# A hybrid trunk layer on one core: the decay's chain of small VectorE operations emitted in five pieces, p read in quarters with a third place, the second half's residual loaded later

## The chip, the core and the metric

The kernel runs on one core of a Trainium2 chip. A core has five engines, each with an instruction stream of its own that it works through in order: TensorE (PE, the matrix products, with its weight loads shown apart as PEld), VectorE (DVE), ScalarE (ACT), GpSimd (POOL) and SyncE (SP, which here only issues transfers). ACT issues transfers too, and sixteen DMA engines carry them between DRAM and the on-chip memory. The metric is the device time of one execution in microseconds; less is better. The kernel before takes 1365.46 us (median of three runs, 1364.79 to 1365.91).

## What is computed

One layer of a decoder trunk over 1024 tokens and 1024 channels, all in float32. The attention group and the gated DeltaNet group read one input projection, their outputs go through `w_o`, and an MLP and a gated embedding follow:

```
u = rmsnorm(h, norm_mix[i])
aq, ak, av, dq, dk, dv, dz, db, da = split(u @ w_in[i])
attn_out = sliding_window_sink_attention(rope(aq), rope(ak), av, sinks)
beta = sigmoid(db)
g = -exp(a_log) * softplus(da + dt_bias)              # the decay
dn_out = chunk_gated_delta_rule(l2norm(silu(conv(dq))) * 128 ** -0.5, l2norm(silu(conv(dk))), silu(conv(dv)), g, beta)
dn_out = rmsnorm(dn_out) * dn_norm * silu(dz)
h = h + concat(attn_out, dn_out) @ w_o[i]
h = h + square(relu(rmsnorm(h, norm_mlp[i]) @ w_up[i])) @ w_down[i]
h = h + sigmoid(rmsnorm(h, norm_ple[i]) @ w_ple_gate[i]) * (p[i] @ w_ple_proj[i])
out = rmsnorm(h, norm_final)
```

## The kernel before

The tokens are worked on in two halves of 512 (`hb` 0 and 1). A product in full precision is made of three passes: each operand is split by `split` (L219 and L220) into a rounded part (a cast on ACT) and its difference to the source (on POOL or DVE), and PE multiplies high by high, high by low and low by high.

*Who sets the order.* Up to w_out, `Flow` writes out two kinds of work. The filler `projections()` is a generator of large GEMMs; the tasks (`prepare`, `chain`, `attend`, and `pairs` with its merges, preps and scans) are chains of small steps, each of which yields the time in microseconds, or the event, for which its next step has to wait. A task that is due goes first, the filler otherwise, and `embed()` is a spare filler for when the filler itself has to wait. That sequence gives the priorities; the scheduler of the tile framework then fixes each engine's own row of instructions by a timeline of its own. On the chip each engine keeps to its row, and an instruction that waits holds back all behind it.

*The decay.* `scalars(s, hb)` (L625 to L672) computes beta and g for a half on tiles of 128x16: some two dozen DVE operations and two exponentials on ACT, a chain in which each needs the one before, written in one piece up to a `yield 3.17`. Three small matmuls of `gg` follow. `norms` adds the l2 norms, and `pre` makes four decay steps: POOL writes `rD` (L724), PE multiplies it by `mgtR`, ACT takes the exponential into `et` (L735), POOL masks it (L737), and DVE multiplies the products of keys and queries by it into `ka` (L751). The key part goes to DRAM (`LD`, L757), comes back as `rD` (L770), and `inverse` (L764 to L784) runs 31 steps on DVE, from L775 to L780. Its result goes through DRAM (`XD`) to `Xt`; `merge` (from L802), `prep` and `scan` follow. The scan carries the state `St` over four chunks for two groups of heads; each link runs through PE, DVE, ACT and POOL, and ends with transposes of `oS` whose split is written to `AT` and `Z`. Two PSUM banks (pool d) serve the scans, three (pool e) all other steps, three (pool g) the filler. `z_gate` (L433 to L437) multiplies z by its silu and the norm's weights, on ACT and in four POOL instructions.

*The embed.* `embed()` (L1049 to L1077) makes p @ w_proj and writes it to the DRAM tensor `PD`. Half of p at a time lies in AT0, as high and low part; a tile of output is 12 matmuls, then ACT copies the bank into `po` (two buffers, L1072) and SP issues the write (L1075). The second half's p can be put into AT0 only when the first half's products are done.

*The residual.* `hT(hb, j)` is where x, transposed, is kept and added to: for the first half the end of `H`; for the second half's first four blocks the beginning of `H`, and AT1 for its last four. `w_out(hb)` begins with two transfers of 1 MB each, issued by ACT (L1006), and adds its products to these places at the end of each group of banks (L1024). For the second half, w_out begins with the part that doesn't need the scan.

Of the kernel before, what the change touches and what calls it, by code (L numbers as in the profile page):

```python
# [18 lines left out]
P = 128  # L19
# [99 lines left out]
def hybrid_block(ctx, tc, t, out):  # L119
# [6 lines left out]
    def nm(s):  # L126
        cnt[0] += 1
        return f"{s}{cnt[0]}"
# [498 lines left out]
    def scalars(s, hb):  # L627

        w = lambda name: dt_([P, 16], name, bufs=2)
        z = ba[:, hb * 4:hb * 4 + 4]  # L630
        v44 = lambda x: x.rearrange("p (t h) -> p t h", t=4)
        beta = w("beta")
        A.activation(v44(beta), z[:, :, 0:4], AF.Exp, scale=-1.0)
        V.tensor_scalar(beta, beta, 1.0, None, op0=ALU.add)
        V.reciprocal(beta, beta)
        a_, e_, f_, g_ = w("sa"), w("se"), w("sf"), w("gg")
        V.tensor_tensor(v44(a_), z[:, :, 4:8], bc(dtb, 1, 4), op=ALU.add)
        V.tensor_scalar(e_, a_, -1.0, None, op0=ALU.mult)
        V.tensor_tensor(e_, e_, a_, op=ALU.min)
        V.tensor_scalar(a_, a_, 0.0, None, op0=ALU.max)  # L640
        A.activation(e_, e_, AF.Exp)

        V.tensor_scalar(f_, e_, 2.0, None, op0=ALU.add)
        V.reciprocal(f_, f_)
        V.tensor_tensor(e_, e_, f_, op=ALU.mult)
        V.tensor_tensor(f_, e_, e_, op=ALU.mult)
        V.tensor_scalar(g_, f_, 1.0 / 17.0, None, op0=ALU.mult)
        for i in (15, 13, 11, 9, 7, 5, 3):
            V.scalar_tensor_tensor(g_, g_, 1.0 / i, f_, op0=ALU.add, op1=ALU.mult)  # L649
        V.scalar_tensor_tensor(g_, g_, 1.0, e_, op0=ALU.add, op1=ALU.mult)  # L650
        V.scalar_tensor_tensor(g_, g_, 2.0, a_, op0=ALU.mult, op1=ALU.add)
        V.tensor_tensor(v44(g_), v44(g_), bc(nea, 1, 4), op=ALU.mult)
        gh = dt_([P, 16], "gh", bufs=2, dt=F32R)
        gl = dt_([P, 16], "gl", bufs=2, dt=F32R)
        A.copy(gh, g_)
        V.tensor_tensor(gl, g_, gh.bitcast(F32), op=ALU.subtract)
        yield 3.17
        b, free = yield from take("e")
        for i, m in enumerate((mle, mgtR.bitcast(F32), ones)):
            T.matmul(b[:, i * 16:i * 16 + 16], m, g_, start=True, stop=True)  # L660
        free()
        ex = dt_([P, 3, 16], "ex", bufs=2)
        A.activation(ex, b[:, 0:48].rearrange("p (i t) -> p i t", i=3), AF.Exp)
        s.update(beta=beta, gh=gh, gl=gl, eG=ex[:, 0], eR=ex[:, 1], eL=ex[:, 2],
                 ss=dt_([P, 2, 16], "ss", bufs=2), KE=[None] * 4, AT=[None] * 4)
        s["LD"] = dram.tile([64, 1024], F32, tag="LD", name=nm("LD"), bufs=2)
        s["XD"] = XD[hb]
        s["BD"] = dram.tile([16, P], F32, tag="BD", name=nm("BD"), bufs=2)
# [330 lines left out]
    def hT(hb, j, n=1):  # L999

        x, o = (H, XW + j * HB) if hb == 0 else (H, j * HB) if j < 4 else (AT[1], (j - 4) * HB)
        return x[:, o:o + n * HB]

    def w_out(hb):
        for j in (0, 4):
            A.dma_start(hT(hb, j, 4).rearrange("p (j s) -> p j s", j=4),  # L1006
                        t["xT"].rearrange("(j p) s -> p j s", p=P)[:, j:j + 4, hb * HB:hb * HB + HB])

        def rhs(b, kt):
            return dn1[b][:, kt - 4] if hb and kt > 3 else uview(R1, b, kt)  # L1010
# [37 lines left out]

    def embed():  # L1049

        for hb in range(2):
            pT = part("AT0", F32R).rearrange("p (b k s) -> p b k s", b=2, k=2)
            for kt in range(2):
                raw = wraw.tile([P, WN], F32, tag="raw", name=nm("pr"))[:, :HB]
                SY.dma_start(raw, t["pT"][kt * P:(kt + 1) * P, hb * HB:(hb + 1) * HB])
                split(pT[:, 0, kt], pT[:, 1, kt], raw, G)
            for g in range(4):
                w = wunit2(t["w_proj"], 0, g * 256, G)
                for m in range(0, 4, 2):
                    ring["g"].n -= 1  # L1060
                    b = bank(ps["g"])
                    for kt in range(2):
                        for i in range(2):
                            for j, (x, y) in enumerate(PASSES):
                                T.matmul(b[:, i * 256:i * 256 + 256],
                                         pT[:, x, kt, (m + i) * P:(m + i + 1) * P],
                                         w[:, y, kt * 256:kt * 256 + 256],
                                         start=kt + i + j == 0, stop=kt * i == 1 and j == 2)
                            if kt + i < 2:
                                yield  # L1070
                    o = cvp.tile([P, HB], F32, tag="cv", name=nm("po"))
                    A.copy(o, b)  # L1072
                    ring["g"].n += 1
                    r = hb * HB + m * P
                    SY.dma_start(PD[r:r + 2 * P, g * 256:g * 256 + 256].rearrange("(i p) c -> p i c", p=P),  # L1075
                                 o.rearrange("p (i c) -> p i c", i=2))
                    yield  # L1077
# [528 lines left out]
```

## Time and profile before

| | |
|---|---|
| median of three runs | 1365.46 us |
| the profiled execution | 1366.2 us, its span 1364.1 us |
| PE busy | 1317.7 us, 97% |
| DVE, ACT, POOL busy | 838.8, 548.0, 434.5 us (61%, 40%, 32%) |
| chain that ended last | PE 74%, DVE 11%, DMA 6%, ACT 3%, POOL 2% |
| decay of the first half, first keys and attention | 50 to 132 us |
| embed, decay steps of the second half | 385 to 448 us |
| w_out, the second half's inverse and scan | 448 to 600 us |

The times of the trace are microseconds from the start of the span. A timeline row gives start, duration, engine, line, operation, what is written and read, and in brackets how long the engine stood idle before it and who released it. Each engine is busy for only part of the time; an idle stretch counts where PE has it. PEclk is the granted clock of PE as a share of 2.4 GHz: 1.00 is the upper level, 0.50 the lower one, 1.2 GHz; a stretch that has both shows a value between.

### The profile page before, as it was taken

The numbers are of one execution on the slowest core, as the hardware profiler recorded it, in microseconds if no ns is written. First come the engines' busy times: TensorE is split into PE (matmuls) and PEld (weight loads), VectorE is DVE, ScalarE is ACT, GpSimd is POOL, SyncE is SP. The second block draws the span as 40 slices with busy tenths as digits, with TensorE's granted clock in tenths as the row PEclk, the third lists the DMA queues.
The fourth block names the chain that finished last, engine by engine and source line by source line (L and its number), as shares of the span: only waits on it lengthen the run. The fifth ranks groups of instructions, "written<-read, shape, count | busy, mean of one in ns | idle before, by whom it ended". The sixth has DMA issues, their size and how long they took to land.

```text
span 1364.1 us, 20392 instructions
## 1 busy us (share of the span) xinstructions
PE 1317.7 (97%) x7664; PEld 1125.5 (83%) x7664; DVE 838.8 (61%) x1558; ACT 548.0 (40%) x1083; POOL 434.5 (32%) x430
## 2 busy tenths in 40 slices
PE   8999999999998999898999999999999999999997
PEld 6788688999897998886788888877888888888886
DVE  6786977697564755797776676654333343344553
ACT  6456375544544433564333333342122231221333
POOL 6673626631385452300011111103122212210332
PEclk9999999999999999999999999999999999999999
DMA  6322222324135431321433323354333333232211
GB/s 223 88 54 73 54 62 52 74 73 105 34 119 176 133 110 33 115 85 63 146 116 116 124 87 114 109 185 136 96 116 101 98 123 120 77 93 73 75 62 47
DMA packets 102738, 134.33 MB, mean 98 GB/s; under 512 B 16400, under 2 KB 71744, under 8 KB 102384
## 3 DMA queue, kind: packets, MB, share of 16 engines
q1 hardware_dynamic: 90528, 110.50, 27.0%
q10 hardware_dynamic: 11760, 21.77, 4.4%
q8 instruction: 60, 0.98, 0.3%
q0 software_dynamic: 352, 0.76, 0.2%
q14 instruction: 38, 0.31, 0.1%
HBM read 106.77 MB, written 26.23 MB: 98 GB/s over the span
## 4 chain that ended last, share of the span: by engine, by line
PE 74%; DVE 11%; DMA 6%; ACT 3%; issue 3%; POOL 2%; SPq 1%; POOLq 0%; ACTq 0%; DVEq 0%
PE bk L102 72%; PE bk L106 2%; DVE w L220 1%; DVE cv L412 1%; DMA AD<-t 1%; ACT w L219 1%; DMA raw<-in_w_in 1%; POOL rsb L358 1%; DMA PD<-po 1%; DMA raw<-in_w_down 1%; DMA H<-in_w_in 1%; DMA AT<-in_xT 0%; DVE gg L649 0%; DMA raw<-AD 0%; SPq L841 0%
## 5 line engine op out<-in xcount | busy, mean ns | idle before, releaser
L102 PE MATMUL bk<-T,w 128*128 128x512 f32 x2304 | 537.9, 392 | 5.7 <-ACT w L219 4.5
L102 PEld LDWEIGHTS bk<-T,w 128*128 128x128 f32 x2304 | 432.8, 188 | 102.6 <-ACT w L219 6.6
L220 POOL TENSOR_TENSOR w<-raw,w 128x512 fp32r<-128x512 f32 x136 | 180.5, 1329 | 621.3 <-ACT w L219 590.2
L219 ACT CAST w<-raw 128x512 fp32r<-128x512 f32 (+1 forms) x280 | 172.6, 620 | 460.8 <-PE bk L102 340.6
L102 PE MATMUL bk<-R,w 128*128 128x256 f32 (+1 forms) x1536 | 240.7, 312 | 1.4 <-ACT w L219 1.4
L102 PEld LDWEIGHTS bk<-R,w 128*128 128x128 f32 x1536 | 210.8, 189 | 22.9 <-issue 2.3
L220 DVE TENSOR_TENSOR w<-raw,w 128x512 fp32r<-128x512 f32 (+1 forms) x144 | 107.5, 748 | 61.1 <-ACT w L219 60.9
L1478 DVE TENSOR_TENSOR H<-bk,H 128x512 f32<-128x512 f32 x96 | 64.6, 690 | 96.0 <-PE bk L102 96.0
L102 PE MATMUL bk<-U,w 128*128 128x512 f32 (+1 forms) x384 | 80.3, 355 | 1.0 <-ACT ba L472 0.6
L102 PEld LDWEIGHTS bk<-U,w 128*128 128x128 f32 x384 | 60.2, 191 | 14.5 <-issue 4.9
L102 PE MATMUL bk<-w,R 128*128 128x256 f32 (+1 forms) x480 | 69.4, 294 | 0.1
L102 PE MATMUL bk<-w,U 128*128 128x256 f32 (+2 forms) x384 | 64.1, 321 | 5.2 <-ACT AT L478 3.2
L102 PE MATMUL bk<-AT,w 128*128 128x256 f32 (+1 forms) x256 | 65.3, 342 | 1.3 <-DVE t L1363 0.8
L102 PEld LDWEIGHTS bk<-w,U 128*128 128x128 f32 x384 | 55.6, 194 | 12.3 <-ACT AT L478 3.4
L102 PEld LDWEIGHTS bk<-w,R 128*128 128x128 f32 x480 | 61.7, 192 | 4.0 <-issue 3.1
L1348 ACT ACTIVATE t<-t 128x512 f32<-128x512 f32 x64 | 40.3, 631 | 39.1 <-DVE t L1347 38.4
L102 PEld LDWEIGHTS bk<-AT,w 128*128 128x128 f32 x256 | 42.8, 191 | 8.3 <-DVE t L1363 1.9
L102 PE MATMUL bk<-R,T 128*128 128x512 f32 (+1 forms) x204 | 48.7, 386 | 0.0
L220 POOL TENSOR_TENSOR T<-ra,T 128x1024 fp32r<-128x1024 f32 x14 | 33.6, 2398 | 46.7 <-ACT T L219 41.0
L102 PE MATMUL bk<-T,T 128*128 128x512 f32 (+1 forms) x204 | 47.0, 379 | 0.0
L555 ACT ACTIVATE s<-s,mx 128x257 f32<-128x257 f32 (+1 forms) x64 | 31.3, 492 | 36.8 <-DVE mx L553 30.2
L102 PEld LDWEIGHTS bk<-T,T 128*128 128x128 f32 x204 | 36.8, 188 | 7.8
(370 smaller groups left out, 1882.1 us busy)
## 6 DMA issues: line engine op xcount, KB each, us to landing
raw<-in_w_in SPq DMA_DIRECT2D x72, 256.0 KB, 2.8
raw<-in_w_up SPq DMA_DIRECT2D x32, 512.0 KB, 4.9
AD<-t ACTq DMA_DIRECT2D x64, 256.0 KB, 2.7
raw<-in_w_down SPq DMA_DIRECT2D x64, 256.0 KB, 3.0
ra<-AD SPq DMA_DIRECT2D x28, 512.0 KB, 4.1
raw<-in_w_o SPq DMA_DIRECT2D x32, 256.0 KB, 3.1
PD<-po SPq DMA_DIRECT2D x16, 256.0 KB, 3.7
rawg<-in_w_gate SPq DMA_DIRECT2D x16, 256.0 KB, 3.2
```

Source lines behind the costliest of these rows:

```text
L102: self.tc.nc.tensor.matmul(o, lh, rh, **k)
L106: self.tc.nc.tensor.transpose(o, x, i)
L219: A.copy(hi, src)
L220: lo_eng.tensor_tensor(lo, src, hi.bitcast(F32), op=ALU.subtract)
L358: eng.tensor_tensor(acc, acc, xr, op=ALU.add)
L412: V.scalar_tensor_tensor(cv if i < 3 else x[:, 3:], x[:, i:i + HB], cw[:, j, i:i + 1], cv, op0=ALU.mult, op1=ALU.add)
L555: A.activation(s[:, i, lo:257], s[:, i, lo:257], AF.Exp, bias=mx[:, i:i + 1], accum_out=sm[:, i:i + 1])
L1348: A.activation(r, r, AF.Square)
L1478: V.tensor_tensor(h, bs[m], h, op=ALU.add)
```

## The change

Three places of the code change. The decay's chain in `scalars` gets four yields of 1.5 us, so that it is written out in five pieces with other work between. p comes in four quarters of 256 tokens; two lie in AT0, the third in a tile of its own (`pT`), the fourth in the first's place; the third is read ahead of the first half's third group of w_proj, the fourth ahead of the second half. For the second half's residual, an 8-column copy on ACT is put ahead of the transfers: it reads a block of the first half's residual and writes into the block to be loaded, so the transfer into `H` waits for that block's first addition, and AT1's transfer is written first.

```diff
@@ scalars
         V.reciprocal(beta, beta)
+        yield 1.5
         a_, e_, f_, g_ = w("sa"), w("se"), w("sf"), w("gg")
...
         A.activation(e_, e_, AF.Exp)
+        yield 1.5
...
         for i in (15, 13, 11, 9, 7, 5, 3):
             V.scalar_tensor_tensor(g_, g_, 1.0 / i, f_, op0=ALU.add, op1=ALU.mult)
+            if i in (13, 7):
+                yield 1.5
@@ w_out
+    def x_in(hb, j):
+        A.dma_start(hT(hb, j, 4).rearrange("p (j s) -> p j s", j=4),
+                    t["xT"].rearrange("(j p) s -> p j s", p=P)[:, j:j + 4, hb * HB:hb * HB + HB])
+
     def w_out(hb):
-        for j in (0, 4):
-            A.dma_start(hT(hb, j, 4).rearrange("p (j s) -> p j s", j=4),
-                        t["xT"].rearrange("(j p) s -> p j s", p=P)[:, j:j + 4, hb * HB:hb * HB + HB])
+        if hb:
+            A.copy(hT(1, 0)[:, 0:8], hT(0, 1)[:, 0:8])
+        for j in (4, 0)[::1 - 2 * (hb == 0)]:
+            x_in(hb, j)
@@ embed
+        two = part("AT0", F32R).rearrange("p (i b s) -> p i b s", i=2, b=2)
+        extra = dx.tile([P, 2, HB], F32R, tag="pT", name="pT")
+        places = [two[:, 0], two[:, 1], extra, two[:, 0]]
+        def quarter(i):
+            raw = wraw.tile([P, WN], F32, tag="raw", name=nm("pr"))[:, :HB]
+            SY.dma_start(raw.rearrange("p (k s) -> p k s", k=2),
+                         t["pT"].rearrange("(k p) s -> p k s", p=P)[:, :, i * 256:i * 256 + 256])
+            split(places[i][:, 0], places[i][:, 1], raw, G)
+        quarter(0)
+        quarter(1)
         for hb in range(2):
-            pT = part("AT0", F32R).rearrange("p (b k s) -> p b k s", b=2, k=2)
-            for kt in range(2):
-                raw = wraw.tile([P, WN], F32, tag="raw", name=nm("pr"))[:, :HB]
-                SY.dma_start(raw, t["pT"][kt * P:(kt + 1) * P, hb * HB:(hb + 1) * HB])
-                split(pT[:, 0, kt], pT[:, 1, kt], raw, G)
+            if hb:
+                quarter(3)
             for g in range(4):
+                if hb == 0 and g == 2:
+                    quarter(2)
                 w = wunit2(t["w_proj"], 0, g * 256, G)
                 for m in range(0, 4, 2):
+                    pT = places[hb * 2 + m // 2]
```

What this does to the engines' rows shows in three places. On POOL, in the decay steps of the second half (`rD` and `et` are a step's tiles, `z` the gating), before:

```order
L724 TENSOR_TENSOR rD_4304<-con,gh_3433 128x512
L724 TENSOR_TENSOR rD_4304<-con,gl_3434 128x512
L944 TENSOR_TENSOR oss_4227<-oss_4227,mhalf 128x2
L437 TENSOR_TENSOR z_3396<-z_3396,rows 128x512 x4
L737 TENSOR_TENSOR et_4301<-et_4301,con 128x512
L220 TENSOR_TENSOR w_5195<-raw_5193,w_5195 128x512
L724 TENSOR_TENSOR rD_4489<-con,gh_3433 128x512
```

The same place on POOL after the change (L728, L741 and L948 are the lines of before, moved down by four):

```order
L728 TENSOR_TENSOR rD_4304<-con,gl_3545 128x512
L741 TENSOR_TENSOR et_4301<-et_4301,con 128x512
L220 TENSOR_TENSOR w_4935<-raw_4933,w_4935 128x512
L728 TENSOR_TENSOR rD_4489<-con,gh_3544 128x512
L728 TENSOR_TENSOR rD_4489<-con,gl_3545 128x512
L220 TENSOR_TENSOR w_4972<-raw_4970,w_4972 128x512
L948 TENSOR_TENSOR oss_4348<-oss_4348,mhalf 128x2
L437 TENSOR_TENSOR z_3396<-z_3396,rows 128x512 x4
L741 TENSOR_TENSOR et_4486<-et_4486,con 128x512
```

The gating stood ahead of the first step's `et`; now it stands ahead of the second's. On ACT, around the transfers into `H` (`x2` is two transfers in a row), before:

```order
L1072 COPY po_5262<-bk_5249 128x512
L959 COPY Z_79<-bk_4458 128x256
L219 CAST w_5325<-raw_5323 128x512
L219 CAST w_5452<-raw_5450 128x512
L1006 DMA H<-in_xT 128x4x512 x2
L913 ACTIVATE oS_4606<-bk_4607,ex_546 128x128 x2
```

The same place on ACT after the change (L739, L1009 and L1095 are L735, L1006 and L1072 of before):

```order
L739 ACTIVATE et_4799<-bk_4796 128x512
L219 CAST AT_4923<-pr_5240 128x512
L1095 COPY po_5216<-bk_5203 128x512
L1009 DMA H<-in_xT 128x4x512
L219 CAST w_5246<-raw_5244 128x512
```

The later transfer on ACT after the change, some thirty rows on in w_out (L1268 squares the first half's new residual, L1015 is the copy):

```order
L219 CAST w_5895<-raw_5893 128x512
L1268 ACTIVATE rsb<-H 128x512
L1015 COPY H<-H 128x8
L1268 ACTIVATE t_6901<-H 128x512
L1009 DMA H<-in_xT 128x4x512
```

One of the two transfers stays at the embed; the other has moved behind w_out's first residual. On PE, near the end of the second half's scan (`St` is the state, `oS` an output that is transposed, `bk_6199` and `bk_6233` the last chunk's banks of the first group of heads), before:

```order
L102 MATMUL bk_6087<-vn_6062,ka_4652 128x128 x2
L102 MATMUL bk_6416<-AT_5500,w_6629 128x256
L102 MATMUL bk_6417<-AT_5500,w_6629 128x256
L106 MATMUL bk_5951<-con,oS_5918 128x128 x2
L102 MATMUL bk_6199<-St_3391,W_6161 128x128 x2
L102 MATMUL bk_6199<-St_3391,xq_2846 128x128 x2
L106 MATMUL bk_6087<-con,oS_6056 128x128
L102 MATMUL bk_6233<-vn_6204,ka_4805 128x128 x2
```

The same links of the scan on PE after the change (just ahead of these rows stand the product of `bk_6087` and five more w_o matmuls):

```order
L102 MATMUL bk_6478<-R_75,w_6541 128x256
L106 MATMUL bk_5951<-con,oS_5918 128x128
L102 MATMUL bk_6478<-R_75,w_6541 128x256
L106 MATMUL bk_5951<-con,oS_5918 128x128
L102 MATMUL bk_6478<-R_75,w_6541 128x256 x4
L102 MATMUL bk_6328<-AT_5500,w_6570 128x256
L102 MATMUL bk_6329<-AT_5500,w_6570 128x256
L102 MATMUL bk_6417<-AT_5500,w_6630 128x256
L102 MATMUL bk_6418<-AT_5500,w_6630 128x256
L102 MATMUL bk_6199<-St_3391,W_6161 128x128 x2
L102 MATMUL bk_6199<-St_3391,xq_2846 128x128 x2
L102 MATMUL bk_6233<-vn_6204,ka_4805 128x128 x2
```

Matmuls of w_out (`R` by `w`) now stand between the links, and the product with `vn` no longer stands behind a transpose of `oS`. The first merge of the second half, where this stretch begins, has 255 w_o matmuls ahead of it in PE's row instead of 321.

## Rows read from the trace of the kernel before

**Rows 1.** The page: busy us, share of the span, instructions of each engine.

```profile
PE 1317.7 (97%) x7664; PEld 1125.5 (83%) x7664; DVE 838.8 (61%) x1558; ACT 548.0 (40%) x1083; POOL 434.5 (32%) x430
```

**Rows 2.** Windows: us, PE, PEld, DVE, ACT, POOL busy, PEclk, DMA share, GB/s.

```profile
406.50:410.50 4.00, 4.00 (x22) 4.00 (x22) 3.17 (x7) 1.38 (x4) 1.32 (x1) 0.57 0.29 47
...
441.00:447.50 6.50, 4.13 (x19) 4.13 (x20) 2.90 (x6) 3.49 (x9) 3.21 (x3) 0.50 0.64 177
450.00:526.00 76.00, 76.00 (x763) 73.22 (x762) 48.76 (x127) 27.79 (x62) 35.40 (x30) 1.00 0.33 95
...
545.00:558.00 13.00, 8.42 (x54) 7.17 (x53) 7.14 (x25) 4.73 (x19) 3.36 (x4) 0.87 0.14 41
```

**Rows 3.** Timeline of PE: start, us, instruction, count [idle before it <- releaser].

```profile
63.43 0.40 PE L102 MATMUL bk<-gg,con 128*128 128x16 f32 x2 [0.60 <-DVE gg L652]
...
89.36 0.37 PE L106 MATMUL bk<-con,s 128*128 128x128 f32 x1 [2.98 <-DVE s L558]
...
406.30 1.56 PE L102 MATMUL bk<-xk 128*128 128x128 f32 x8 [2.03 <-DVE ka L751]
...
420.19 0.92 PE L102 MATMUL bk<-vn,ka 128*128 128x128 f32 x4 [2.52 <-ACT oS L913]
...
427.87 1.05 PE L102 MATMUL bk<-xk 128*128 128x128 f32 x8
...
443.37 5.10 PE L102 MATMUL bk<-w,AT 128*128 128x256 f32 x24 [3.77 <-ACT po L1072]
...
448.45 2.62 PE L102 MATMUL bk<-R,w 128*128 128x256 f32 x20
...
451.72 35.94 PE L102 MATMUL bk<-R,w 128*128 128x256 f32 x301
487.59 0.68 PE L102 MATMUL bk<-XT,ka 64*64 64x64 f32 x16
```

**Rows 4.** Timeline of POOL, first half's weights, then the second half's decay.

```profile
68.47 1.32 POOL L220 TENSOR_TENSOR w<-raw,w 128x512 fp32r<-128x512 f32 x1 [1.76 <-ACT w L219]
...
395.84 5.11 POOL L437 TENSOR_TENSOR z<-z,rows 128x512 f32<-128x512 f32 x4
400.90 1.30 POOL L737 TENSOR_TENSOR et<-et,con 128x512 f32<-128x512 f32 x1
```

**Rows 5.** Timeline of ACT (ACTq: a transfer that it issues).

```profile
392.06 1.28 ACT L735 ACT_TABLE_LOAD   x1
...
393.36 0.60 ACT L735 ACTIVATE et<-bk 128x512 f32<-128x512 f32 x1
...
430.07 0.98 ACTq L1006 DMA_DIRECT2D H<-in_xT  x2
```

**Rows 6.** Transfers from 424 to 450 us: issuer, count, KB each, us to landing.

```profile
H<-in_xT ACTq DMA_DIRECT2D x2, 1024.0 KB, 9.4
```

**Rows 7.** The tile po, 385 to 450 us: landing of its 14 writes.

```profile
DMA to landing us min/median/max: 2.1/3.4/10.1
```

**Rows 8.** Timeline of DVE: the inverse's start, a residual addition, the transpose.

```profile
446.69 1.22 DVE L775 TENSOR_TENSOR rD<-rD,bS 128x1024 f32<-128x1024 f32 x1
...
460.28 0.69 DVE L1024 TENSOR_TENSOR H<-bk,H 128x512 f32<-128x512 f32 x1 [1.11 <-PE bk L102]
...
486.31 0.45 DVE L802 STREAM_TRANSPOSE XT<-Xt 128x256 f32<-128x256 f32 x1 [1.83 <-DMA Xt<-XD]
```

**Rows 9.** Waits of PE from 526 to 560: us in total, times, longest.

```profile
PE bk L106 <- DVE oS L949: 2.3, 2, 1.2
PE bk L102 <- DVE kvs L858: 1.9, 2, 1.4
PE bk L102 <- DVE Z L220: 1.8, 2, 0.9
```

**Rows 10.** Timeline of SP's issues: the loads rD<-LD.

```profile
437.99 4.73 SPq L770 DMA_DIRECT2D rD<-LD  x2
```

More of the change, by code (lines that the diff above doesn't have):

```diff
@@ L1065, in embed @@
                                 T.matmul(b[:, i * 256:i * 256 + 256],
-                                         pT[:, x, kt, (m + i) * P:(m + i + 1) * P],
+                                         pT[:, x, kt * 256 + i * P:kt * 256 + i * P + P],
                                          w[:, y, kt * 256:kt * 256 + 256],
```

## The prediction

> **What bounds the kernel now.** I read the busy times first: PE works 1317.7 us of the span of 1364.1 [rows 1], so at most 46 us of idle time can be won, and with them the stretches behind a long gap in which the granted clock is at its lower level. DVE, ACT and POOL are each idle for a third of the span or more; they matter only where PE waits for them. So the change is priced at PE's gaps, in the stretches where the order differs: 50 to 132 us, 345 to 380, 385 to 452 (the embed and the second half's decay steps) and 452 to 600 (w_out and the second half's scan). From 132 to 345 us and behind 600 every engine has the rows that it had.
>
> Second I read PE's own instructions with the waits ahead of them [rows 3]. In the stretch of the embed there are three: 2.03 us for `ka` (DVE L751), 2.52 for `oS` (ACT L913) and 3.77 for `po` (ACT L1072). Behind each the windows show the lower level, 1.2 GHz for 2.4: a mean of 0.57 over 406.5 to 410.5 us, which with PE busy all 4.00 us loses 0.43 x 4.00 = 1.7 us (the stretch behind 420.3 is alike), and 0.50 over 441 to 447.5, where PE is busy for 4.13 us and loses half of that, 2.1 [rows 2]. From 450 to 526 PE has no gap at all. Then, where the filler has run out, waits come again: 2.3 us for `oS`, 1.9 for `kvs`, 1.8 for `Z` [rows 9], and 0.87 of the clock over 13.00 us, another 1.7 [rows 2].
>
> **The sum, part by part**, against the profiled execution (1366.2 us; its span and 2.1 us around it).
>
> *The residual of the second half, later.* Of the wait of 3.77 us for `po` the row on the transfers tells the cause: ACT issues two loads of `H`, 1024 KB each, at 430.07 [rows 5]; they take 9.4 us to land [rows 6], and one PD write takes 10.1 where the median is 3.4 [rows 7]. ACT's `po` copy needs that write's buffer back, PE needs the copy's bank. The change leaves one of the two loads there; the other comes behind the copy L1007, which needs the first result of w_out(0), some 40 us later, when nothing waits for it: its data are first added at the end of w_out. Two loads in 9.4 us are 4.7 each, so the slow write should land after about 5.4 us, 2.0 above the median. Wait and slow clock are 3.77 + 2.1 = 5.9 us. At best all goes; at worst none (the writes, `w_o`, LD and rD still share the engines). I take that 1.6 stays: **-4.3**. The copy itself is one 128x8 instruction on an ACT that has just squared 128x512 beside it, and PE never waits for it: 0.
>
> One rule speaks against this part. The row shows an early transfer that harms. The Trainium skill (DMA: Bandwidth & Descriptors, "Rules for kernel authors") advises to issue a DMA early and wait for it late; by that alone the later load could win nothing, and this term would be 0 instead of -4.3 (the total -2.7); that case lies among the slow writes below. The measured 10.1 us against 3.4 speaks for the term.
>
> *p in quarters with a third place.* The same bytes in as many transfers, and as many casts and POOL differences; PE's 192 embed matmuls are the same. The second half's first quarter no longer waits until the first half is through with AT0. None of PE's waits in this stretch is for `AT`, so by itself 0. But with the pieces below it changes where the embed stands: it starts later, and after the `ka` matmuls of the last decay step 100 embed matmuls are left ahead of w_out where 72 were: 28 x 0.12 = 3.4 us of cover (301 matmuls of this shape take 35.94 us [rows 3], 0.12 each).
>
> *The decay steps of the second half.* Their order on POOL moves the gating of z (four instructions, 5.11 us [rows 4]) from ahead of the first step's `et` to ahead of the second's. Before, `et` came at 400.90, right behind the gating, and PE waited 2.03. Now the first `et` is free, and the second stands behind a difference, an `oss` and the gating, while the PE rows that wait for its banks come after some 28 embed matmuls. On ACT the silu of z now splits two exponentials: two more table loads, 1.28 us each, with the next `et` 1.30 behind the load's start [rows 5]: 2.6 us of ACT on the way to `et`. So the gap at this place moves and does not go. Bounds: both old waits gone with their slow clock (-8), or z and `et` (5.11 + 1.30) waited for in full in place of 2.03 (+4.4). With one stall removed and one made of the same work, nearest is **0**.
>
> The rows show 1.30 us from load to next start. The Trainium skill (ScalarE: Activation LUTs, "What ACT_TABLE_LOAD costs") puts a drain on top, 2.66 us for every switch; by that the term would be +2.7 and the total -4.3. The trace disagrees: ACT starts again as the load ends.
>
> *The tail.* The first merge of the second half stands 66 w_o matmuls earlier in PE's row (255 stand ahead of it where 321 did): 66 x 0.12 = 7.9 us of filler move into the scan, where PE had waited. The pairs of transposes and kvs products, bare before, get 31 w_o matmuls between them: the 1.9 us go. Some 15 of them stand between the last update of St and the next read of it, which covers one of the two waits for `Z` (0.9). And the product with `vn` no longer queues behind the transpose that waits for `oS`: one of two (1.2). That is **-4.0** of 6.0 [rows 9]; the last links of the scan have nothing behind them and stay, with their slow clock. Bounds 0 and -7.7 (6.0 + 1.7).
>
> *The price of the earlier merge.* PE had no slack there: DVE's transpose of Xt was done at 486.31 + 0.45 [rows 8] and PE took it at 487.59 [rows 3], without a wait. From the first w_o matmul (448.45) that was 39.1 us; now PE is there after 31.2. DVE needs 39.6 from L775 (446.69) to the transpose, less two residual additions and two sums that now stand behind the inverse, with their waits some 4.5 us [one such: rows 8]: about 35. So L775 must start about 4 us ahead of the first w_o matmul; before it was 1.8. From the `ka` matmuls at 427.87 it took 18.8 us to L775, and rD<-LD sat in SP's queue from 437.99 on while the loads ran [rows 10]; with one load (4.7) less, 14.1. PE takes 20.6 - 5.9 + 3.4 = 18.1 from there to w_out, plus what stays of the wait. That gives the 4 us, just. Bounds: 0, and if nothing gets faster for LD and rD, 4.6. I take **+1.3**.
>
> *The first half's chain.* It keeps its DVE place; the `gg` matmuls go some 5 us back on PE, so the wait of 0.60 at 63.43 goes [rows 3]. In exchange POOL ropes ahead of three differences for the next GEMM, 1.32 us each [rows 4]: up to 3.9 us of new waiting. Both lie ahead of the wait of 2.98 at 89.36 for DVE's `s` (L558), and DVE is what sets that time, so what PE loses before it gets back there. Bounds -0.6 and +0.9; **0**. In the second half DVE's rows of this chain stand where they stood: five pieces or one is the same there. The other reorderings (345 to 380 us) lie where PE waits for nothing.
>
> Sum: -4.3 + 0 - 4.0 + 1.3 + 0 = -7.0 us, so 1359.2 in an execution like the profiled one. That one lies 0.7 above the median of 1365.5, so 1358.5.
>
> **Rivals.** *The inverse comes late* (slower). The gating of z stands on POOL ahead of the second `et`; if PE's three banks of that pool are all taken, PE stands for 5.11 + 1.30 us (+4.4 and 1.7 at the low clock), the remaining decay steps, LD and the inverse slide with it, and PE reaches the merge long before DVE: 4.6 and 2.1 more. 6.1 + 6.7 - 4.3 - 4.0 = +4.5: 1370.0. It decides once the wait at the second decay step is over some 6 us. For it: POOL's row above. Against it: before, the same four instructions cost only 2.03.
>
> *The PD writes are slow by themselves.* With two `po` buffers a round of two costs a copy and a landing, 0.6 + 3.4 us, while PE makes two in 24 x 0.12 = 2.9. If that, and not the load, sets the wait, only about 1 of the 5.9 us goes: -1.0 - 4.0 + 1.3 = -3.7, 1361.8. Against it: PE went through the first half's eight such tiles with no wait for `po`.
>
> *The waits only move.* The scan's last part is a chain through ACT, DVE, POOL and PE; filler that is put between its links may run while the chain is ready and leave the same gaps at the end. Then -4.3 + 1.3 and a new slow stretch of 1.7: -1.3, 1364.2. This is also the case in which the change does not do what it says.
>
> **How the numbers follow.** Forecast 0.48; better than it, with the decay step's waits gone too (near 1353), 0.07; slow writes 0.17; waits only move 0.17; late inverse 0.11. A measurement of this kernel can tell about 0.2%, 2.7 us, from no change: 1362.7 and 1368.2 are the borders. Faster: 0.48 + 0.07 + most of the slow writes (0.13) + a little of the waits (0.02) = 0.70; same 0.19; slower 0.11. The range leaves out the slower rival and the best part of the gains: 1353 to 1366.
>
> **What would show it.** Right: no PE wait for `po` over 2 us and full clock at the embed's end, PD writes below 6 us; one wait of 2 to 4 us at a decay step, now for the second `et`; the kvs waits gone, with waits for `oS` and `Z` below 3 us; PE at the first merge waiting under 2 us for DVE. Wrong: a wait of over 4 us ahead of the merge or for the banks of w_out's second group, PE waiting on POOL's differences at 74 to 80 us with 89 later than before, or `po` waits that stay with a single load in flight.

## The result and the profile after

The changed kernel takes 1378.05 us (median of six runs, 1372.28 to 1378.51) against 1365.87 us for the kernel before (1364.79 to 1369.34): a ratio of 1.0085, interval 1.0071 to 1.0100. It is slower by 12 us, where 7 us less were forecast. The profiled execution has a span of 1376.3 us, 12.2 more than before. The page, as in [rows 1]:

```profile
PE 1322.7 (96%) x7664; PEld 1127.4 (82%) x7664; DVE 836.1 (61%) x1558; ACT 552.0 (40%) x1086; POOL 434.1 (32%) x430
```

PE is busy for 5.0 us more with the same 7664 matmuls, so 7 of the 12 us are waiting; in the other 5 the same matmuls took longer, slow clock among the reasons (a mean granted clock of 0.984 for 0.987). Where they arise is read with one measure in all that follows: the columns that PE's matmuls stream are added up from the start, and for each point the time at which a kernel has reached as many columns as the kernel before is compared. In stretches of equal work, named by the times of the kernel before (us longer than before; the last column is the whole span, with 0.3 us ahead of 50 us in it):

| kernel, profiled execution | 50-132 | 132-345 | 345-385 | 385-450 | 450-526 | 526-600 | behind | span |
|---|---|---|---|---|---|---|---|---|
| the change | +5.7 | +1.0 | +0.5 | +0.6 | +6.2 | -2.6 | +0.4 | +12.2 |
| predicted | 0 | 0 | 0 | -4.3 | +1.3 | -4.0 | 0 | -7.0 |

The borders at 385 and 526 us lie among rows whose order changed; counted by matmuls in place of columns, the stretches beside them move by up to 2.2 us. And one profile differs from another where the rows are the same: pieces_first, below, has the rows of the kernel before from 132 us on, and its profile is 3.4 us shorter from 385 to 450.

Half of the loss is in the first half's attention, where the forecast had nothing. The waits of PE there, as [rows 3]:

```profile
72.59 0.40 PE L102 MATMUL bk<-gg,con 128*128 128x16 f32 x2 [1.23 <-DVE kL L220]
76.91 1.21 PE L102 MATMUL bk<-w,R 128*128 128x256 f32 x8 [0.79 <-POOL w L220]
80.77 0.75 PE L102 MATMUL bk<-w,R 128*128 128x256 f32 x4 [1.97 <-POOL w L220]
83.47 0.47 PE L102 MATMUL bk<-kH,qT 128*128 128x128 f32 x1 [1.95 <-DVE qT L529]
99.98 0.39 PE L102 MATMUL bk<-kH,qT 128*128 128x256 f32 x1 [1.92 <-DVE qT L529]
```

Before, this stretch had one wait of 2.98 us, for `s`, with slow clock behind it, and one of 0.60 for `gg` [rows 3]. Now there are five waits, 7.9 us together, and slow clock behind two of them (windows of the changed kernel: us, PE, PEld, DVE, ACT, POOL busy, PEclk, DMA share, GB/s):

```profile
83.40:87.20 3.80, 3.73 (x18) 3.73 (x19) 3.67 (x7) 2.81 (x5) 2.06 (x6) 0.55 0.28 69
100.00:104.20 4.20, 4.20 (x18) 3.11 (x19) 3.02 (x11) 3.47 (x13) 0.21 (x1) 0.59 0.02 6
```

What these waits hang on is seen on POOL, ACT and DVE of the changed kernel:

```profile
75.58 1.27 POOL L220 TENSOR_TENSOR w<-raw,w 128x512 fp32r<-128x512 f32 x1
...
79.46 1.26 POOL L220 TENSOR_TENSOR w<-raw,w 128x512 fp32r<-128x512 f32 x1
...
82.30 1.27 POOL L220 TENSOR_TENSOR w<-raw,w 128x512 fp32r<-128x512 f32 x1 [0.22 <-ACT w L219]
```

```profile
81.60 0.62 ACT L219 CAST w<-raw 128x512 fp32r<-128x512 f32 x1 [7.93 <-DMA raw<-in_w_in]
82.13 0.57 ACT L528 CAST qT<-bk 64x512 fp32r<-64x512 f32 x1
```

```profile
82.73 0.68 DVE L529 TENSOR_TENSOR qT<-bk,qT 64x512 fp32r<-64x512 f32 x1 [5.83 <-ACT qT L528]
```

POOL does its ropes first, so the first difference comes at 75.58 where it came at 68.47 [rows 4]. The difference is the last reader of the raw weight, and there are two raw buffers: the third load can start only behind it. ACT's cast of that load stands idle for 7.93 us, `qT`'s cast stands right behind the cast, and DVE stands idle for 5.83 us. In the kernel before the cast had waited 2.24 us, and DVE did the same subtraction at once (ACT, then DVE):

```profile
72.64 0.62 ACT L219 CAST w<-raw 128x512 fp32r<-128x512 f32 x1 [2.24 <-DMA raw<-in_w_in]
...
75.54 0.69 DVE L529 TENSOR_TENSOR qT<-bk,qT 64x512 fp32r<-64x512 f32 x1
```

Of the rest 4.8 us lie between 345 and 600 us, most of them behind 450. The waits of PE that answer to [rows 3], in the changed kernel:

```profile
400.58 0.47 PE L102 MATMUL bk<-rD,mgtR 128*128 128x512 f32 x1 [0.81 <-DVE kd L865]
402.74 0.50 PE L102 MATMUL bk<-w,AT 128*128 128x256 f32 x2 [1.18 <-ACT w L219]
409.49 0.47 PE L102 MATMUL bk<-rD,mgtR 128*128 128x512 f32 x1 [1.16 <-ACT et L739]
...
419.42 0.79 PE L102 MATMUL bk<-xk 128*128 128x128 f32 x2 [2.45 <-DVE ka L755]
...
449.39 1.68 PE L102 MATMUL bk<-w,AT 128*128 128x256 f32 x12 [1.60 <-ACT po L1095]
...
488.31 0.68 PE L102 MATMUL bk<-XT,ka 64*64 64x64 f32 x16 [0.71 <-DVE XT L806]
502.72 0.68 PE L102 MATMUL bk<-ka,X 64*64 64x64 f32 x8 [2.64 <-DVE X L832]
```

The wait for `po` has shrunk from 3.77 to 1.60 us, and those for `kvs` are gone, as forecast. Four waits have come at the embed and the decay steps (5.6 us) in place of two (2.03 and 2.52), and two at the merges, where PE had none; behind the second of these the clock is slow (the window, as above):

```profile
503.40:506.90 3.50, 3.19 (x16) 3.22 (x17) 2.14 (x5) 1.00 (x2) 0.30 (x1) 0.52 0.32 82
```

### The profile page after: what moved, and what is told of

The parts are those of the page before. It is cut to its first block, busy times and chain, and to the rows that moved or that the text cites. A ratio compares the mean times of both kernels' runs of the same rounds, so it can differ in the third digit from the quotient of the medians.

```text
span 1376.3 us, 20398 instructions
## 1 busy us (share of the span) xinstructions
PE 1322.7 (96%) x7664; PEld 1127.4 (82%) x7664; DVE 836.1 (61%) x1558; ACT 552.0 (40%) x1086; POOL 434.1 (32%) x430
## 4 chain that ended last, share of the span: by engine, by line
PE 72%; DVE 9%; DMA 8%; ACT 4%; issue 3%; POOL 3%; SPq 0%; POOLq 0%; DVEq 0%; ACTq 0%
PE bk L102 70%; PE bk L106 2%; DMA raw<-in_w_o 2%; ACT w L219 1%; DVE w L220 1%; DMA raw<-in_w_proj 1%; DMA raw<-in_w_down 1%; POOL w L220 1%; POOL rsb L358 1%; DMA AD<-t 1%; DMA H<-in_w_in 1%; DVE cv L412 1%; DMA AT<-in_xT 0%; DMA raw<-in_w_up 0%; DMA Xt<-XD 0%
## 5 line engine op out<-in xcount | busy, mean ns | idle before, releaser
L102 PE MATMUL bk<-w,R 128*128 128x256 f32 (+1 forms) x480 | 72.5, 299 | 2.8 <-POOL w L220 2.8
```

The lines of the kernel that those rows point to most:

```text
L102: self.tc.nc.tensor.matmul(o, lh, rh, **k)
```

## The experiments

Each kernel is the kernel before with the edit shown, or the change where that is said. Ratios are against the kernel before on the same chip, with their intervals. Not all kernels ran on one chip, so they are compared by these ratios.

### Which part loses

Pieces in one half alone (`if not hb` or `if hb` ahead of each new yield), the two other parts without pieces, and the residual alone.

```diff
+        if not hb:
+            yield 1.5
```

> The kernel before with the four yields in the first half's decay only. Theory A: the first half's pieces alone carry the 5.7 us that the changed kernel has lost by 132 us: POOL's weight differences come behind the ropes, so the two buffers of raw weights come free late, ACT stands at the next weight's cast waiting for its transfer, and the queries' cast behind it holds up DVE. Then 1371.6 (5.7 over before), with an ACT wait of 7 to 8 us for raw<-in_w_in near 81 us and a DVE wait of over 5 us for qT. Rival B (my prediction's step): DVE sets 89 us whatever stands on POOL; then within 1 us of before, 1365 to 1367.

> The kernel before with the four yields in the second half's decay only. The order puts the gating of z ahead of the second et, and 240 w_o matmuls ahead of the first merge where before has 321. Theory A: PE now reaches the merges before DVE; waits of 3 to 5 us there with a stretch at the low clock, the po wait stays, the kvs waits go: 1366 to 1371, and nothing lost by 132 us. Rival B (the prediction): the filler in the scan wins 4 us and the merge costs 1.3: 1362 to 1364.

> The changed kernel without the four yields: p in quarters and the later residual alone. The order leaves the gating of z where it was before, and has 337 w_o matmuls ahead of the first merge (before 321). Theory A: both losses of the changed kernel come from the pieces, and what the other two parts do is the gain at the po wait: 1358 to 1363. Rival B: the parts that were to help lose too, by the other order of the embed: 1366 to 1370.

> The kernel before with the second half's residual loaded later, and nothing else. Theory A: the PE wait of 3.77 us for po and the low clock behind it come from the two loads of 1 MB; with one of them gone the PD writes land in under 6 us and 3 to 5 us go: 1361 to 1363. Rival B: two po buffers and the writes' own time set the wait; then 1364 to 1366, with a wait for po of over 2.5 us.

| kernel | median us | ratio | interval |
|---|---|---|---|
| pieces_first | 1370.1 | 1.0028 | 1.0014 to 1.0042 |
| pieces_second | 1370.3 | 1.0026 | 1.0012 to 1.0040 |
| no_pieces (quarters, residual) | 1362.3 | 0.9981 | 0.9957 to 1.0005 |
| resid_only | 1368.2 | 1.0013 | 1.0001 to 1.0026 |

The pieces lose, in either half. pieces_first repeats the first half's loss: PE is 5 to 6 us late from 113 to 340 us, and some of that comes back later. The later residual wins nothing by itself: `po` is still waited for, 3.9 us in two waits for 3.77 in one, though the slowest PD write takes 7.2 us for 10.1. Together with the quarters no `po` wait over 0.3 us is left in no_pieces, whose interval reaches just over 1.

### Pieces, or a delay

One piece, and the yield behind it raised by the 6.0 us that the four new yields add up to.

```diff
-        yield 3.17
+        yield 9.17
```

> The decay's chain in one piece as before, and the one yield behind it raised from 3.17 to 9.17, which is the sum of the yields of the five pieces (4 x 1.5 + 3.17). The rows that this gives on PE, DVE, ACT, POOL and SP are those of the five pieces (without quarters and residual). Theory A (the pieces do nothing but put off what follows them by 6 us of the planner's time): the loss of both halves' pieces, 3.8 + 3.5 us: 1372 to 1375 us, with PE late by about 5.7 us from 124 to 340 us and later still after 400. Theory B (it is the cutting, by what DVE does between the pieces): 1364 to 1368 us.

1370.9 us, ratio 1.0030 (1.0013 to 1.0048). The rows that it gives on all five engines are those of the pieces in both halves, line by line but for the buffers' numbers, and that is the stronger result: the cuts do nothing, and the change's first part is a delay of what follows the chain. Theory A holds, but its size doesn't: by the ratios the two halves alone lose 3.8 and 3.5 us, and both together 4.1, not 7.3. So the whole change, 12 us, is not the sum of its parts either (no_pieces lost nothing).

### The first half: the raw ring

The eight weight loads of the second half's query GEMM get places in `H`, which is idle then: once in the kernel before, once with pieces_first.

```diff
-    def wunit2(src, k2, c0, lo_eng=None, n=256):
-        raw = wraw.tile([P, WN], F32, tag="raw", name=nm("raw"))[:, :2 * n]
+    def wunit2(src, k2, c0, lo_eng=None, n=256, raw=None):
+        if raw is None:
+            raw = wraw.tile([P, WN], F32, tag="raw", name=nm("raw"))[:, :2 * n]
...
+                           raws=lambda i: H[:, XW + i * 512:XW + i * 512 + 512])
```

> The kernel before, with one thing added: the eight weight loads of the second half's query GEMM (L1093) get places of their own in H, which is idle there, in place of the ring of two raw buffers. It is the control of raws_first. In the trace of before no PE wait between 65 and 85 us is for a weight, so both theories expect about no change: 1364 to 1368 us, and a PE row like before's up to 100 us. More than 3 us either way would show that the early loads disturb other things, and then only the difference of the two kernels counts.

> The five pieces in the first half alone (1370.1 us as measured before, PE 5 to 6 us late from 113 us on), with the same places in H for the eight loads. POOL still ropes ahead of the weight differences, but no load waits any more for a raw buffer that POOL has yet to read. Theory A (the raw ring: late POOL difference, late load, ACT's cast waits for it 7.93 us with qT's copy behind it, DVE idle for 5.83 us): against raws_before the delay at 124 to 340 us falls from 5.7 to under 2 us, DVE's wait for qT at 82 us goes, and the total is within 2 us of raws_before. Theory B (the POOL differences are themselves late, the ring is only a symptom): PE still waits 1 to 3 us in two or three places for w from POOL, and the delay stays at 3.5 us or more.

raws_before: 1364.5 us, 0.9992 (0.9976 to 1.0008). raws_first: 1365.2 us, 1.0001 (0.9985 to 1.0017), where pieces_first had 1.0028. Against raws_before PE is 2.9 us late at 82 us, and from 110 to 340 us within 0.5 of it (the change is 4.8 to 7 late there against the kernel before). The rows of raws_first, PE and DVE:

```profile
77.16 2.72 PE L102 MATMUL bk<-w,R 128*128 128x256 f32 x14 [2.33 <-POOL w L220]
90.57 0.41 PE L106 MATMUL bk<-con,s 128*128 128x128 f32 x2 [0.83 <-DVE s L559]
```

```profile
75.28 0.68 DVE L530 TENSOR_TENSOR qT<-bk,qT 64x512 fp32r<-64x512 f32 x1
```

POOL's difference is still late and PE still waits 2.33 us for it. But DVE is not held, and what PE lost there comes back at the wait for `s`, which is 0.83 where raws_before has 2.16. That is the argument of the prediction, and it holds once the load has a place. So the ring of two buffers is what made the delay cost in this half.

### The second half: the merge's place

The change, and its merges of the second half emitted later; 360 w_o matmuls stand ahead of the first, where the change has 255 and the kernel before 321.

```diff
             yield start
+            if hb:
+                yield 52.0
```

> The changed kernel with one line more: the second half's merges are emitted 52 us later, so that 360 w_o matmuls stand ahead of the first of them on PE where the change has 255 and before had 321. Theory A (PE comes to the merge 5 us too early for DVE: waits 0.71 for XT, 2.64 for X, and 1.7 of slow clock behind them): these go, the delay between 477 and 510 us against the kernel before no longer grows by 7, and at most 2 to 4 us come back at the scan's end, where 105 fewer matmuls (11 to 12 us of PE work) are left: 1371 to 1375 us. Theory B (the loss lies ahead of it, in the decay steps and z's gating, and the merge waits only show it): the wait moves into the tail, 1377 to 1380 us.

1378.4 us, 1.0099 (1.0065 to 1.0134): nothing won. Up to 508 us the delay no longer grows, as theory A had it (1.9 us at 476 and 1.2 at 508, where the change goes from 7.8 to 15.8), but it grows behind: from 450 to 600 us the change lost 3.6 us, this kernel 7.5 (5.2 up to 526 us). The wait for `X` has not gone, it has become two (its rows of PE):

```profile
507.61 0.50 PE L102 MATMUL bk<-ka,X 64*64 64x64 f32 x5 [1.49 <-DVE X L832]
519.91 0.68 PE L102 MATMUL bk<-ka,X 64*64 64x64 f32 x8 [1.66 <-DVE X L832]
```

Why is seen in the change itself, on DVE (first two rows) and SP:

```profile
500.80 0.45 DVE L806 STREAM_TRANSPOSE XT<-Xt 128x256 f32<-128x256 f32 x1 [4.60 <-DMA Xt<-XD]
502.24 0.43 DVE L832 TENSOR_TENSOR X<-bk,bb 64x256 f32<-64x256 f32 x1
```

```profile
488.38 7.81 SPq L281 DMA_DIRECT2D raw<-in_w_o  x4
496.30 1.83 SPq L845 DMA_DIRECT2D Xt<-XD  x4
```

On DVE the step `X` of one merge stands behind the transpose of a later one, which waited 4.60 us for its load. SP issued this load at 496.30, right behind four weight loads that took SP from 488.38 to 496.19; in the kernel before it issued it at 492.86 and the transpose waited 0.36. So the merges have an order of their own on DVE and SP that goes where they go. That SP's queue is what held the load is read from the rows; moving the load to another queue was not tried.

### The second half: the gating of z

The second half's gating on DVE in place of POOL, in the kernel before and in pieces_second.

```diff
-    def z_gate(zz):
+    def z_gate(zz, eng=G):
...
-            z_gate(z1[0])
+            z_gate(z1[0], V)
```

> The kernel before with the second half's gating of z on DVE in place of POOL (z_gate(z1[0]) at L996 with VectorE); no pieces. Its first merge of the second half has 240 w_o matmuls ahead of it and 96 embed matmuls follow the last ka, as in the kernel with pieces in the second half (240 and 96), though nothing is delayed. It is the control of zdve_second and a test by itself. Theory A (the second half loses by the earlier merge): 1369 to 1372 us, a wait for X of 2 us or more. Theory B (it loses by decay steps behind the gating on POOL): 1363 to 1367 us.

> The five pieces in the second half alone (1370.3 us) with z's gating on DVE. Theory A (the earlier merge): no better than pieces_second, 1369 to 1373 us. Theory B (z's gating on POOL, 5.13 us, stands ahead of the second et, and the decay steps slide with it): the delay that pieces_second built up at 385 to 420 us (5.7 us) falls to under 2, no wait for ka over 2 us there, 1364 to 1368 us and within 2 us of zdve_before.

zdve_before: 1360.0 us, 0.9953 (0.9937 to 0.9968), the lowest ratio here. zdve_second: 1359.1 us, 0.9955 (0.9932 to 0.9977). Their first merges have 240 and 210 w_o matmuls ahead of them, and that did not make them slow: theory A falls. The second `ka` step in pieces_second (POOL, then DVE) and with the gating on DVE (zdve_second):

```profile
401.79 5.13 POOL L437 TENSOR_TENSOR z<-z,rows 128x512 f32<-128x512 f32 x4
406.87 1.27 POOL L743 TENSOR_TENSOR et<-et,con 128x512 f32<-128x512 f32 x1
```

```profile
412.54 1.28 DVE L757 TENSOR_TENSOR ka<-bk,et 128x512 f32<-128x512 f32 x2
```

```profile
400.61 2.50 DVE L437 TENSOR_TENSOR z<-z,rows 128x512 f32<-128x512 f32 x4 [1.44 <-ACT z L434]
406.62 1.27 DVE L757 TENSOR_TENSOR ka<-bk,et 128x512 f32<-128x512 f32 x2
```

`ka` comes 5.9 us sooner; the inverse starts at 433.95 for 443.27. In the kernel before the gain is as plain (zdve_before): the inverse starts at 429.95 where it started at 446.69 [rows 8], its result is transposed at 471.57 for 486.31, and no wait for `ka` over 0.5 us is left.

```profile
429.95 1.23 DVE L775 TENSOR_TENSOR rD<-rD,bS 128x1024 f32<-128x1024 f32 x1 [2.95 <-DMA rD<-LD]
...
471.57 0.45 DVE L802 STREAM_TRANSPOSE XT<-Xt 128x256 f32<-128x256 f32 x1 [0.41 <-DMA Xt<-XD]
```

The gating on POOL cost the kernel before some 6 us already, which [rows 4] had shown as 5.11 us right ahead of `et`. Whether the pieces' own loss (3.5 us) is gone with it, these two alone can't tell, since their intervals leave 4 us either way; the trace has zdve_second 5.1 us behind zdve_before at 450 us and ahead of it from 550 on. The next group tells more.

### The whole change, mended

The change with the gating on DVE; with that and the places for the raw loads; and the change without the later residual.

> The whole change with the second half's gating of z on DVE in place of POOL; the first half as in the change. Theory A (the loss of the second half is the decay steps behind z's gating on POOL): PE is 5 to 6 us late from 124 us on as in the change, but the 6 us that the change lost between 345 and 600 us become a gain of 3 to 7: 1363 to 1368 us. Theory B (a third cause in the pieces together with quarters or residual): 1371 us or more.

> The whole change with both mends: the eight weight loads of the second half's query GEMM in places of their own in H, and the second half's gating of z on DVE. If the two causes are all there is, the change is harmless now and what is left is the gain of the gating with that of quarters and residual: 1357 to 1361 us, no delay over 2 us at 124 to 340 us. If a third cause stays: 1364 us or more.

> Five pieces and quarters, with both residual loads where they were. Pieces alone were 1370.9 (as one delay), the whole change 1378. Theory A (quarters are no help once the embed starts late: first weight and first et waited for): 1373 to 1378 us, so the residual does nothing here. Theory B (the residual's two ACT instructions or its second load do the harm together with the pieces): 1368 to 1371 us.

| kernel, against before | 50-132 | 132-385 | 385-450 | 450-526 | 526-600 | ratio | interval |
|---|---|---|---|---|---|---|---|
| the change | +5.7 | +1.6 | +0.6 | +6.2 | -2.6 | 1.0085 | 1.0071 to 1.0100 |
| no_resid | +5.6 | +3.1 | -4.2 | +3.5 | +3.0 | 1.0085 | 1.0059 to 1.0112 |
| after_zdve | +3.4 | +1.0 | -8.5 | +1.8 | -3.0 | 0.9997 | 0.9977 to 1.0016 |
| after_mended | +1.1 | +0.3 | -7.2 | +1.6 | -2.0 | 0.9963 | 0.9944 to 0.9982 |

With two edits that leave the change as it is, all of its loss goes: 1378.1, 1364.7 and 1360.2 us. The gating gives the change 0.88% (12 us), where it gives the kernel before 0.47% (6.4 us): the 5.6 us between would be the change's own loss behind the gating, if the two gains simply added. The raw places give another 0.34%, 4.6 us. That would place 10 of the change's 12 us; the next group shows that the gating's worth depends on the order around it, so the 5.6 is argued and only the sum of the two mends is shown. Nor does the mended change win: the kernel before with the gating on DVE alone has 0.9953, the change with both mends 0.9963. The later residual plays no part in the loss (no_resid 1377.8 us). What stays open is why the quarters, which lose nothing without the delay (quart_only below, 0.9990), cost 7.5 us with it (no_resid 1.0085 for delay_only 1.0030).

### Do the gains add up

Quarters alone; quarters and residual with the yield lowered from 3.17 to 1.5; this with the gating on DVE (zdve_np_1p5); and this and after_mended with a later merge (`yield 48.0` at the place of late_merge52, 306 w_o matmuls ahead of it).

> p in quarters alone; the decay in one piece and both residual loads where they were. With the residual the quarters gave 1362.3, and the residual alone 1368.2. Theory A (the quarters carry the gain, since the embed no longer stands still between its halves and the po writes are spread): no wait for po over 1 us though both 1 MB loads are there, 1361 to 1364 us. Theory B (the two need each other: the loads still delay a PD write to about 10 us): a po wait of 2 to 4 us stays, 1365 to 1368 us. My prediction had 0 for this part by itself.

> Quarters and later residual with the decay in one piece (1362.3 us, ratio 0.998 with an interval that touched 1), and the yield behind it lowered from 3.17 to 1.5, the other way than the pieces went. In the second half nothing moves by that; in the first half what follows the chain is emitted earlier. If a delay of that chain is what costs in the first half, less of it costs nothing and may win up to 1 us; otherwise it is a repeat of the two parts: 1360 to 1364 us, ratio 0.996 to 0.9995.

> Quarters and later residual, the decay in one piece with the yield of 1.5 (1361.0 us, 0.9964), and the second half's gating of z on DVE (by itself 1360.0 us, 0.9953). Both take PE's waits at 400 to 450 us (ka, oS, po: 8.3 us with slow clock behind them), so they can't add up in full: 1355 to 1360 us, ratio 0.992 to 0.996. If the filler that is won only leaves the scan's end bare, no better than one of them alone: 1360 to 1362.

> zdve_np_1p5 (1366.7 us) with the second half's merges emitted 48 us later, so that 306 w_o matmuls stand ahead of the first of them where 278 stood. Theory A (PE is at the merge before DVE's inverse: 4.2 us for X, 1.0 for XT, 1.7 of slow clock): 28 matmuls are 3.4 us, so 3 to 6 us come back, 1360 to 1364 us, waits for X below 2 us. Theory B (these waits are the chain's own latency and go where the merge goes): 1365 to 1368 us with X waited for as long, later.

> after_mended (1360.2 us; 0.9 us of wait for XT at the merge, none for X) with the merges later in the same way, 306 w_o matmuls ahead for 263. Theory A and B both give little: 0.9 us for XT at most to win, and 43 matmuls (5 us of work) less behind the merge, which the scan's end would miss: 1359 to 1364 us. Below 1358 would mean that a later merge is good in any order; above 1365 that the merge's place costs far more than its waits show.

| kernel | median us | ratio | interval |
|---|---|---|---|
| quart_only | 1365.0 | 0.9990 | 0.9972 to 1.0008 |
| np_1p5 | 1361.0 | 0.9964 | 0.9948 to 0.9981 |
| zdve_np_1p5 | 1366.7 | 1.0004 | 0.9988 to 1.0021 |
| np_late48 | 1365.8 | 0.9984 | 0.9969 to 0.9999 |
| mended_late48 | 1362.3 | 0.9975 | 0.9957 to 0.9992 |

In quart_only `po` waits of 2.47 and 1.83 us stay, as theory B had it, though its slowest PD write takes 7.1 us and not 10. With the later residual they are gone in no_pieces, but np_1p5 has 2.1 us of them again, so what sets them is not settled. np_1p5 shows a gain, its interval below 1; its rows on PE differ from those of no_pieces between 320 and 390 us and at the scan's end, and what the shorter yield has in the gain was not separated. But 0.9964 and 0.9953 make 1.0004, not 0.992: PE of zdve_np_1p5 is 6.9 us ahead of the kernel before at 480 us and 2.7 behind at 500, with these waits over the whole second half:

```profile
PE bk L102 <- DVE X L828: 4.2, 3, 2.5
PE bk L106 <- DVE oS L949: 3.8, 5, 1.1
PE bk L102 <- ACT po L1091: 3.7, 1, 3.7
```

The merge put later (np_late48) takes the wait for `X` away and brings 2.1 us of `kvs` and longer waits for `Z` and `oS` in its place:

```profile
PE bk L106 <- DVE oS L949: 4.3, 5, 1.1
PE bk L102 <- ACT po L1093: 2.8, 1, 2.8
PE bk L102 <- DVE Z L220: 2.5, 3, 0.9
PE bk L102 <- DVE kvs L858: 2.1, 2, 1.3
```

By the measure above PE of np_late48 is 7.2 us ahead of zdve_np_1p5 at 526 us and 2.4 at 600. By the ratios neither kernel with a later merge differs clearly from the one without: 0.9984 for 1.0004, and where PE waited little at the merge, 0.9975 for 0.9963 (mended_late48). The waits thus speak for one stock of filler, in which the tail pays for what the merge saves; the times alone don't show it.

## Why the prediction was wrong, point by point

Forecast and profile lie 19.2 us apart, in three steps that failed and one that fell short: the first half's chain (5.7), embed and decay steps (5.4), the earlier merge (4.9) and the tail (1.4). The remaining 1.7 lie in the other stretches.

*The first half's chain (0, bounds -0.6 to +0.9; measured +5.7).* The failed step is "DVE is what sets that time, so what PE loses before it gets back there". The ropes ahead of the differences were seen and priced at 3.9 us, and the late differences came as said. But the step took DVE's time as given. It asked who waits for POOL on PE and not what else POOL holds: the raw buffer, with it SP's next load, ACT's cast and what stands behind that cast. In part the step came true even so: PE was 8.1 us late at 82 us and 3.3 at 94, behind the wait for `s`. But 98 us finds it 8.2 late again, for the next `qT`. raws_first shows that the step is right where the load has a place of its own.

*The decay steps of the second half (0, bounds -8 to +4.4).* The failed step is "the gap at this place moves and does not go", with 0 for it. From 345 to 450 us the change is 1.1 us late in all, though the `po` wait and its slow clock gave back 4.3 there; so the decay steps and the embed's late start cost 5.4, beyond the upper bound of +4.4. after_zdve gives 9.1 us back in the stretch from 385 to 450 alone. The rival of the late inverse had the right row, the gating ahead of the second `et`, and with 1370.0 the nearest time, but not by its own condition: it asked for a wait of over 6 us at the second decay step, and the longest there is 2.45.

*The residual (-4.3).* In the change the `po` wait of 1.60 us is what the prediction said would stay, the slow clock there is gone, and the slowest write of the embed takes 5.3 us for 10.1. In that kernel the term was right. Its cause was not: with the load moved and nothing else, 3.9 us of waits stayed. That was the sign that the prediction named for being wrong here. It speaks for a share of the rival of writes that are slow by themselves, and for another of the quarters, costed at 0; no run separates the two. The Trainium skill's advice to issue a transfer early (DMA: Bandwidth & Descriptors, "Rules for kernel authors") is not refuted by these runs: the later load alone, 1.0013, won nothing.

*The earlier merge (+1.3, bounds 0 to 4.6).* Mis-sized, +6.2 from 450 to 526. The inverse started 8.4 us ahead of the first w_o matmul, not 4; but DVE took 39.9 us from L779 to the transpose, not the 35 of the estimate, and the wait for `X` behind SP's queue was not thought of. Waits of 0.71 and 2.64 with 1.5 of slow clock (0.48 of 3.19) are 4.9 of it.

*The tail (-4.0; measured -2.6 from 526 to 600).* The way was right. The `kvs` waits went, `Z` and `oS` were 1.9 for 4.1; but a new one of 1.7 for `oss` came, and slow clock took more (the window that answers to the last of [rows 2], 3.4 us lost for 1.7 by the prediction's reckoning):

```profile
559.23 0.71 PE L102 MATMUL bk<-vn,ka 128*128 128x128 f32 x4 [1.73 <-DVE oss L949]
```

```profile
549.00:575.00 26.00, 21.92 (x158) 20.53 (x158) 11.81 (x38) 9.88 (x33) 7.31 (x8) 0.87 0.17 49
```

The two terms, merge and tail, were taken as two effects; together they were to win 2.7 us and lost 3.6. The waits of np_late48 speak for one stock of filler, which can be spent once.

*The chances.* The slower outcomes had 0.11. The row of the gating and the ropes were both in the text; neither was followed past the engine that PE waits for.

## What to carry to other kernels

In a program whose order a planner writes out, a new yield is first of all a delay: make the same delay without the cuts and compare the rows before anything is said of the cuts. Where an engine's step moves back, list what it holds besides its result: the buffer it reads last, the transfer that waits for that buffer, and each queue that stands behind that transfer. Gains that all come from filler ahead of one chain need not add up (here 0.9964 and 0.9953 made 1.0004), so price the chain's own start (here the inverse) and not the waits one by one.

## What was not expected

The gating of z, four operations on 128x512, took POOL 5.11 to 5.13 us and DVE 2.50 us in zdve_second, but 4.59 in zdve_before. And moving it wins 6.4 us, more than its own length: the inverse then starts 16.7 us sooner, since the gating stood on the way to each later decay step. How much of the 16.7 is the planner's other order, which came with the move, was not separated.

A single profile differs from another in stretches that the change does not touch: behind 600 us, where PE has the same work, the kernels here lie between 2.9 us shorter and 2.7 us longer than the kernel before. The medians decide; a profile alone can't tell 3 us.
